# Gathering the first expert group's rows of two tiles in float32, straight from the residual sum

## The chip, the cores and the metric

The kernel runs on one core of a Trainium2 chip. The metric is the device time of one execution in microseconds: the median of several runs. Smaller is better.

## The reference

One layer of a hybrid decoder on 256 prompt tokens and 8 sample tokens, width 1024, all float32. What matters here is its second half:

```python
hres = x + jnp.concatenate([att, conv_y], axis=-1) @ w_out
hn = rmsnorm(hres, g_ffn)
...
lg = (x @ w_rg) + b_rg;  g = jnp.argmax(lg, axis=-1)        # hier_moe(x = hn): 4 groups
le_g = ((x @ w_re) + b_re) of group g                      # 8 experts in each
top_l, top_i = lax.top_k(le_g, 2); w_top = softmax(top_l) * softmax(lg)[g]
h = silu(x @ w_gate[e]) * (x @ w_up[e]) * gates[:, e]       # for each of 32 experts e
y = hres + sum_e h @ w_down[e]
```

The last result is `rmsnorm(y, g_final)`. The weights of the 32 experts are 3 MiB each, 96 MiB in all.

## The kernel before, in words

**Tiles of rows.** The 264 token rows lie in `yres` (128 partitions x 3 x 1024): tiles 0 and 1 are prompt rows, tile 2 the 8 sample rows. They are handled in the order 0, 2, 1, since tile 1's attention and output projection end last.

**The order written out by hand.** `ORDER` (lines 36 to 46) lists named steps; each step is a small function in `steps`, and they are issued in that order, on all engines at once. So each engine works its instructions off in the order of the list. The last three lines of the list hold the stretch that the change touches. Steps that the prediction names, with t the tile, k a column piece, hf a half of the columns:
- `o111`, `o112` and the like (`out_mm`, lines 749 to 760): output projection of tile 1, added to `yres` on VectorE. `o111` and `o112` are the two halves of its last block and write the same PSUM tile.
- `Htk` (`norm2_half`, lines 796 to 820): sum of squares on ScalarE, transposes on TensorE into `xh` with the norm's weight (VectorE), and the float32r rounding `hn` of the rows (ScalarE).
- `Otk` (`norm2_lo`, line 827): the remainder `hlo` = row minus `hn`, on VectorE, for tile 2 on GpSimd. A product with `hn` and one with `hlo` give the float32 result in two float32r products.
- `ltk`, `Rt`, `R1p`, `Lt`: router logits on TensorE, the norm's scale (VectorE, then a power on GpSimd), logits times scale.
- `rat` to `ret` (`route`): the routing in five parts on VectorE. `rct` gives `A` (which two experts a row goes to), `rdt` starts two exponentials on ScalarE, `ret` ends with the gates `G`.
- `rkt`, `oht`: the rank of a row among its expert's rows (TensorE), and the one-hot `Pg` of the slots of the first expert group (VectorE).
- `g00` to `g21` (`gather_mm`, line 987; first digit the tile, second the half of the columns; `h` or `l` behind them is one of the two float32r products): product of one-hot and rows into `px`, so that the 4 x 32 slots of the group get their rows. `ga0` and `ga1` copy the halves of `px` to `xr` (ScalarE and VectorE, lines 998 and 1000), `gt0` and `gt1` transpose them and scale them to `xg` (lines 1016 to 1022).
- `warmi` (`fill`, line 1063): products whose result nobody reads.
- `room` (line 1071): tiles for the weights that are loaded in pieces.

`hn` and `hlo` hold the columns in the order in which the experts' weights want them (eight planes of 128), the residual sum in natural order, so that rounding and remainder also permute. In column order of the weights, neighbours lie 8 floats apart in `yres`.

**Experts.** The 32 experts go in 8 groups of 4. For each group: gate product `pgt` and up product `pup` (line 1149), the gather of the next group (line 987, from `hn` and `hlo`, all tiles), the down product `pyy` (line 1163), and its way back into `yres` (lines 1171 to 1257). Beside the first gate product run `gather_rs` (the slots' scale, `prs`, line 1007) and `slot_maps` (`PGw` on GpSimd, line 1126, which needs `G` and is read by a product on TensorE ahead of the up product).

**Weights.** SyncE issues the loads in a fixed order (lines 1095 to 1122), 1 MiB each, into a ring of 15 slots; a load waits until the last product that read its slot has ended. Group 1's gate weights g10 to g13 take the four slots of the output-projection weights. u02 and u03 (experts 2 and 3, up, group 0) don't go into the ring but in pieces into the tiles `uq` and `uh` that `room` made; u11 goes half into `uh` and half into the slot of g00. In the kernel before, SyncE's order is: group 0 (gate, two up, down), g10 to g13, u02, u03, u10, the two halves of u11, u12, u13, d10 and so on.

Of the kernel before, what the change touches and what calls it, by code (L numbers as in the profile page):

```python
# [85 lines left out]
def hymba_step(ctx: ExitStack, tc: tile.TileContext, x_prompt, x_sample, cache_k, cache_v, state_conv,  # L86
# [35 lines left out]
    with tc.manual_schedule():  # L122
# [673 lines left out]
        def norm2_half(t, k):  # L796

            n = NR[t]
            a, w = COLS[t][k]
            if k == 0:  # L800
                hn[t] = c4(f"hn{t}", [128, 8, 128], F32R)
                if t == 2:

                    P.memset(hn[t][0:40].bitcast(F32), 0.0)
                    hlo[t] = hn[t][32:40]
                else:
                    hlo[t] = c4(f"hlo{t}", [128, 8, 128], F32R)
                ss2[t] = c1(f"ssb{t}", [128, 3])
                xh[t] = c4("xh", [128, 8, 128])
            y = yres[:n, t, a:a + w]  # L810
            S.activation(sqj[:n, 0:w], y, AF.Square, accum_out=ss2[t][:n, k:k + 1])
            pt = ps("pt")
            pv_ = pt.rearrange("p (c n) -> p c n", c=4)
            m, c0 = w // 128, a // 128
            for c in range(m):
                T.transpose(pv_[:, c, 0:n], y[:, 128 * c:128 * c + 128], ident[:n, :n])
            V.tensor_tensor(xh[t][:, c0:c0 + m, 0:n], pv_[:, 0:m, 0:n],
                            gfT[:, c0:c0 + m, None].to_broadcast([128, m, n]), op=OP.mult)
            p = slice(a // 8, (a + w) // 8)
            S.copy(hn[t][:n, :, p].rearrange("t c p -> t p c"), y.rearrange("t (p c) -> t p c", c=8))  # L820

        def norm2_lo(t, k):

            n = NR[t]
            a, w = COLS[t][k]
            p = slice(a // 8, (a + w) // 8)
# [238 lines left out]
        for i in range(3):  # L1065
            steps[f"warm{i}"] = lambda: fill(2)
# [342 lines left out]
```

## Time and profile before

| | us |
|---|---|
| runs, median of 3 | 422.75 |
| lowest and highest | 421.94, 424.46 |
| profiled execution, its own time | 423.49 |
| its span | 421.8 |
| TensorE busy in the span | 382.7 (91%) |
| VectorE, ScalarE, GpSimd busy | 196.4, 92.0, 104.7 |

The span runs from the first to the last instruction of the profiled execution; its own time is 1.7 us longer. In the profile PE is TensorE, PEld its weight loads, DVE is VectorE, ACT ScalarE, POOL GpSimd, SP SyncE, and SPq the queue in which SyncE issues transfers; L987 is line 987 of the kernel. A float32 product of 512 columns appears as two instructions, one of float32r as one. The engines' shares are means over stages with different limits, so they are read stage by stage.

### The profile page before, as it was taken

To read this page: it belongs to the slowest core of one execution; us is meant where nothing else is said; L and a number is where in the kernel's file an instruction comes from. 1 tells how busy PE (TensorE), PEld (TensorE's weight loads), DVE (VectorE), ACT (ScalarE), POOL (GpSimd) and SP (SyncE) were. 2 spreads that over 40 slices of the span, in tenths; PEclk is the share of its full clock that TensorE was granted. 3 is DMA by queue.
4 is the path that set the end of the run, shared out by engine and by line. 5 is a ranking of instruction groups with operands and counts; after the bars stand their busy time and mean duration, and the time that the engine had idled before them with its cause. 6 is when DMAs were issued, how large, how long until landed. Compare 5 with 4: busy or idle time off the path is not lost.

```text
span 421.8 us, 6576 instructions
## 1 busy us (share of the span) xinstructions
PE 382.7 (91%) x2626; PEld 208.0 (49%) x2626; DVE 196.4 (47%) x384; ACT 92.0 (22%) x232; POOL 104.7 (25%) x103
## 2 busy tenths in 40 slices
PE   7899999999999999987999999888699699799980
PEld 6354346678775334464545554443353364354530
DVE  2148987899764033688234343406015016024054
ACT  4120223164340012241320212111011021011032
POOL 3636888978306001030100000000000000000041
PEclk9899999999999999999899999989889789799996
DMA  7999978869987999949699999999999999999922
GB/s 259 416 373 421 367 292 308 340 220 392 424 358 266 421 429 423 409 204 347 234 413 399 425 427 425 426 428 424 428 427 424 427 427 426 427 427 416 401 99 108
DMA packets 32981, 155.04 MB, mean 368 GB/s; under 512 B 3068, under 2 KB 5322, under 8 KB 17972
## 3 DMA queue, kind: packets, MB, share of 16 engines
q1 hardware_dynamic: 27328, 119.69, 70.1%
q0 software_dynamic: 5008, 33.80, 20.3%
q10 hardware_dynamic: 612, 1.11, 0.7%
q8 instruction: 22, 0.36, 0.3%
q14 instruction: 11, 0.09, 0.1%
HBM read 152.40 MB, written 2.20 MB: 367 GB/s over the span
## 4 chain that ended last, share of the span: by engine, by line
PE 42%; DMA 32%; DVE 13%; issue 7%; POOL 3%; ACT 1%; DVEq 0%; ACTq 0%; SPq 0%; POOLq 0%
DMA u<-in_w_up_dram 14%; DMA g<-in_w_gate_dram 9%; DMA d<-in_w_down_dram 8%; PE py L755 4%; PE pup L1149 4%; PE pov L709 3%; PE acck L238 3%; DVE Sd L480 3%; PE accB L552 3%; PE pgt L1149 3%; PE accq L238 3%; PE pyy L1163 3%; PE accv L238 2%; PE px L987 2%; POOL K L474 1%
## 5 line engine op out<-in xcount | busy, mean ns | idle before, releaser
L1149 PE MATMUL pup<-u,xg 128*32 128x256 f32 x472 | 42.9, 468 | 12.2 <-DMA u<-in_w_up_dram 12.2
L1223 DVE SCALAR_TENSOR_TENSOR sh<-pup,rsl,sh 128x256 f32<-128x256 f32 x8 | 5.3, 666 | 90.2 <-PE pup L1149 83.6
L1126 POOL TENSOR_TENSOR PGw<-Pg,G 128x384 f32<-128x384 f32 x8 | 6.9, 857 | 161.0 <-DVE Pg L976 124.4
L474 POOL TENSOR_TENSOR K<-K,qv 128x2048 f32<-128x2048 f32 x9 | 40.7, 4536 | 6.3 <-DMA K<-in_cache_k_dram,idx 4.5
L480 DVE TENSOR_REDUCE Sd<-K 128x32 f32<-128x2048 f32 x16 | 35.9, 2277 | 4.7 <-POOL K L474 4.6
L1149 PE MATMUL pgt<-g,xg 128*32 128x256 f32 x512 | 32.5, 394 | 3.5 <-DMA g<-in_w_gate_dram 2.4
L1149 PEld LDWEIGHTS pup<-u,xg 128*32 128x32 f32 x472 | 19.2, 133 | 32.0 <-DMA u<-in_w_up_dram 16.3
L1163 PE MATMUL pyy<-d,hT 128*32 128x512 f32 (+1 forms) x272 | 30.9, 579 | 0.6 <-DVE hT L1243 0.6
L755 PE MATMUL py<-wo,mixT 128*128 128x512 f32 (+1 forms) x72 | 29.0, 550 | 1.1 <-DVE yres L760 1.1
L1180 PE MATMUL pz<-Y,PT 128*128 128x512 f32 (+1 forms) x90 | 26.7, 421 | 0.7
L1149 PEld LDWEIGHTS pgt<-g,xg 128*32 128x32 f32 x512 | 16.5, 113 | 18.4 <-DMA g<-in_w_gate_dram 3.8
L1257 DVE TENSOR_TENSOR yres<-yres,pz 128x512 f32<-128x512 f32 (+1 forms) x42 | 25.6, 670 | 0.0
L1172 DVE SCALAR_TENSOR_TENSOR Y<-pyy,gsl,Y 128x512 fp32r<-128x512 f32 (+1 forms) x17 | 12.2, 720 | 25.5 <-ACT Y L1171 25.5
L998 ACT COPY xr<-px 128x512 f32<-128x512 f32 (+1 forms) x16 | 8.8, 557 | 68.0 <-PE px L987 68.0
L987 PE MATMUL px<-hn,Pg 128*128 128x512 f32 (+1 forms) x48 | 21.9, 480 | 0.1
L1171 ACT ACTIVATE Y<-pyy,gsl 128x512 fp32r<-128x512 f32 (+1 forms) x17 | 11.3, 663 | 48.3 <-PE pyy L1163 48.3
L1180 PEld LDWEIGHTS pz<-Y,PT 128*128 128x128 f32 (+1 forms) x90 | 12.1, 154 | 18.0 <-ACT Y L1171 6.4
L303 POOL DMA_INDIRECT V<-in_cache_v_dram,idx x16 | 15.1, 944 | 22.2 <-PE pov L709 18.2
L755 PEld LDWEIGHTS py<-wo,mixT 128*128 128x128 f32 x72 | 13.3, 190 | 13.5 <-issue 11.8
L303 POOL DMA_INDIRECT K<-in_cache_k_dram,idx x16 | 15.7, 982 | 12.4 <-DMA K<-in_cache_k_dram,idx 5.6
L1163 PEld LDWEIGHTS pyy<-d,hT 128*32 128x32 f32 x272 | 8.3, 111 | 17.7 <-issue 16.1
L238 PE MATMUL accq<-wq,xnT 128*128 128x512 f32 x32 | 16.3, 657 | 0.3 <-DVE xnT L221 0.3
(334 smaller groups left out, 612.0 us busy)
## 6 DMA issues: line engine op xcount, KB each, us to landing
g<-in_w_gate_dram SPq DMA_DIRECT2D x32, 1024.0 KB, 19.6
d<-in_w_down_dram SPq DMA_DIRECT2D x28, 1024.0 KB, 19.6
u<-in_w_up_dram SPq DMA_DIRECT2D x25, 1024.0 KB, 19.5
u<-in_w_up_dram SPq DMA_DIRECT2D x9, 512.0 KB, 14.2
wo<-in_w_out_dram SPq DMA_DIRECT2D x4, 1024.0 KB, 15.1
wk<-in_w_in_dram SPq DMA_DIRECT2D x2, 1024.0 KB
wv<-in_w_in_dram SPq DMA_DIRECT2D x2, 1024.0 KB, 30.6
wC<-in_w_in_dram SPq DMA_DIRECT2D x2, 1024.0 KB
```

What stands on the lines that cost most here:

```text
L238: T.matmul(acc, lhsT=xnT[:, cc, 128 * t:128 * t + 128], rhs=W[pn, kk][:, c, :], start=cc == 0, stop=cc == 7)
L303: P.indirect_dma_start(out=t, out_offset=None, in_=src, in_offset=bass.IndirectOffsetOnAxis(ap=idx[:, b, hh:hh + 1], axis=0))
L474: P.tensor_tensor(kslots[i], kslots[i], qv[:, None, :].to_broadcast([128, 4, 512]), op=OP.mult)
L480: V.tensor_reduce(Sd[:, b, 4 * hh:4 * hh + 4, :].rearrange("p i h -> p (i h)"), kslots[i].rearrange("p i (h d) -> p (i h) d", h=8), axis=A ...
L552: T.matmul(acc[:, 0:264], lhsT=W[pn, kk][:, c, 128 * m:128 * m + 128], rhs=xnT[:, cc, 0:264], start=cc == 0, stop=cc == 7)
L709: T.matmul(po[32 * j:32 * j + 32], lhsT=pvs[b // 4][:, b % 4, i, :], rhs=vslots[2 * b + i // 4][:, i % 4, :], start=s == 0, stop=s == 1, t ...
L755: T.matmul(po[:, lo:lo + w], lhsT=mixT[:, c, 128 * t:128 * t + 128], rhs=wo[n, c // 4][:, c % 4, lo:lo + w], start=c == 0, stop=c == 7, sk ...
L987: T.matmul(PX[grp, hf], lhsT=PgS[grp][:n, POS[t]].rearrange("p j s -> p (j s)"), rhs=(hn, hlo)[low][t][:n, 4 * hf:4 * hf + 4, :].rearrange ...
L1149: T.matmul(dst[32 * j:32 * j + 32, 0:256], lhsT=xg[:, c, 32 * j:32 * j + 32], rhs=w[:, 256 * k:256 * k + 256], start=c == 0, stop=c == 7, ...
L1163: T.matmul(py[32 * j:32 * j + 32, 0:w], lhsT=hT[:, c, 32 * j:32 * j + 32], rhs=dw[grp, j][:, 1024 * c + a:1024 * c + b], start=c == 0, sto ...
L1180: T.matmul(pz, lhsT=PTS[grp][:, 128 * t:128 * t + NR[t]], rhs=Y[:, i, 0:w], start=start and i == 0, stop=i == 1, skip_group_check=more)
L1257: V.tensor_tensor(yv, yv, pz[:m], op=OP.add)
```

## The change

For tiles 1 and 2 the rows of the first expert group are gathered by float32 products straight from `yres`, read in the weights' column order (stride 8). Tile 0 still uses `hn` and `hlo`. The rounding and remainder of tiles 2 and 1, which the later groups use, become two steps `hl2` and `hl1` at the end of the list (ScalarE and VectorE, two pieces of 512 columns each; none on GpSimd any more). In the list `re0` moves up behind `rd0`, `re2` and `re1` behind `gt1`; `H12` is cut in two and `R1` is put between the parts; three pairs of warm-up products become a pair and a single one. On SyncE u02 and u03 are loaded ahead of g13 in place of behind it.

```diff
-H21 l20 R2 g00 O20 l21 O21 L2 ra2 rb2 room g01 o111 rc2 l10 O10 o112 H11 R1p H12 rk2 oh2 R1 O11 l11 l12 L1 ra1 rb1 rc1
-g20 warm0 g21 warm1 rk1p rk1 warm2 oh1 O12 rd2 g10h g11h re0 g10l ga0 g11l ga1 re2 gt0 gt1 rd1 re1
+H21 l20 R2 g00 l21 L2 ra2 rb2 room g01 o111 rc2 l10 o112 H11 R1p H12a R1 H12b rk2 oh2 l11 l12 L1 ra1 rb1 rc1
+g20 warm0 g21 rk1p rk1 warm1 oh1 rd2 g10 ga0 g11 ga1 gt0 gt1 rd1 re2 re1 hl2 hl1
...
+            return pv_
+        def norm2_x(t, k, pv_):
...
             V.tensor_tensor(xh[t][:, c0:c0 + m, 0:n], pv_[:, 0:m, 0:n],
                             gfT[:, c0:c0 + m, None].to_broadcast([128, m, n]), op=OP.mult)
-            p = slice(a // 8, (a + w) // 8)
-            S.copy(hn[t][:n, :, p].rearrange("t c p -> t p c"), y.rearrange("t (p c) -> t p c", c=8))
+            if t == 0:
+                norm2_hi(t, a, w)
+        def norm2_hi(t, a, w):
+            n, p = NR[t], slice(a // 8, (a + w) // 8)
+            S.copy(hn[t][:n, :, p].rearrange("t c p -> t p c"),
+                   yres[:n, t, a:a + w].rearrange("t (p c) -> t p c", c=8))
+        def norm2_both(t):
+            for a in (0, 512):
+                norm2_hi(t, a, 512)
+                norm2_lo(t, a, 512)
...
-            (P if t == 2 else V).tensor_tensor(
+            V.tensor_tensor(
                 hlo[t][:n, :, p], yres[:n, t, a:a + w].rearrange("t (p c) -> t c p", c=8),
                 hn[t][:n, :, p].bitcast(F32), op=OP.subtract)
...
+                steps["H12a"] = lambda: late.append(norm2_half(1, 2))
+                steps["H12b"] = lambda: norm2_x(1, 2, late[0])
+            if t:
+                steps[f"hl{t}"] = lambda t=t: norm2_both(t)
...
             for t in tiles:
+                if grp == 0 and t:
+                    n = NR[t]
+                    T.matmul(PX[grp, hf], lhsT=fl(PgS[grp], t, n).bitcast(F32),
+                             rhs=yres[:n, t, :].rearrange("t (p c) -> t c p", c=8)[:, 4 * hf:4 * hf + 4, :],
+                             start=False, stop=t == 1)
+                    continue
...
-        for i in range(3):
-            steps[f"warm{i}"] = lambda: fill(2)
+        for i in range(2):
+            steps[f"warm{i}"] = lambda i=i: fill(2 - i)
...
                 for j in range(4):
+                    if (grp, nm, j) == (1, "g", 3):
+                        for k in (2, 3):
+                            load_split(0, "u", k, uw, wu_v)
...
-                if (grp, nm) == (1, "g"):
-                    for j in (2, 3):
-                        load_split(0, "u", j, uw, wu_v)
```

## Rows read from the trace of the kernel before

**Rows 1.** Busy time by stretch: stretch, its length, then for PE, PEld, DVE, ACT and POOL busy us and (instructions), then the granted TensorE clock (1.00 is 2.4 GHz, 0.50 is 1.2 GHz), the DMA engines' busy share and GB/s.
```profile
184.00:189.00 5.00, 3.86 (x22) 3.17 (x21) 4.69 (x14) 1.03 (x3) 1.67 (x2) 1.00 0.07 26
204.00:207.00 3.00, 3.00 (x39) 1.95 (x31) 0.00 (x0) 0.59 (x2) 0.43 (x1) 1.00 0.10 30
212.00:222.00 10.00, 9.76 (x63) 5.16 (x63) 3.32 (x6) 2.70 (x5) 0.00 (x0) 1.00 1.00 399
242.00:400.00 158.00, 141.56 (x1234) 73.06 (x1230) 44.91 (x73) 21.09 (x46) 4.17 (x5) 0.91 1.01 424
```

**Rows 2.** The waits of SyncE's queue over the whole run: engine line, waited for what: us in total, times, longest us. (The first is the wait for the slot of the last output-projection weight; the row names the next instruction on TensorE that signalled.)
```profile
SPq L1110 <- PE pt L816: 12.3, 3, 11.9
...
SPq L1081 <- PE pgt L1149: 10.1, 1, 10.1
```

**Rows 3.** The timeline of SyncE, its issues: start us, us over all, engine line operation, out<-in, count.
```profile
189.26 2.04 SPq L1081 DMA_DIRECT2D uq<-in_w_up_dram  x4
...
205.53 0.33 SPq L1081 DMA_DIRECT2D u<-in_w_up_dram  x1
```

**Rows 4.** The chain of waits, pieces in order of time: start us, us, what.
```profile
156.53 3.44 PE py L755 x8
...
200.48 5.03 PE pgt L1149 x64
...
207.72 3.59 PE pup L1149 x64
211.31 3.29 PE px L987 x10
```

**Rows 5.** The timeline of VectorE: start us, us, engine line operation, out<-in, shapes, count, and in brackets, where there was any, the idle time before it and what ended it. The routing of the sample tile (183 to 185 us), the last piece of tile 1's second norm and what stands behind it (190 us), the same two routing steps for tile 1 (192 us), and the first and last of the eight instructions of gate step re0 and the first of re2's.
```profile
183.10 1.12 DVE L899 SCALAR_TENSOR_TENSOR rcols<-L,rcols,tab 128x4 f32<-128x4 f32 x1
...
184.45 1.27 DVE L906 SCALAR_TENSOR_TENSOR l<-rcols,L 128x32 f32<-128x32 f32 x1
...
189.80 0.42 DVE L817 TENSOR_TENSOR xh<-pt,rowsT 128x256 f32<-128x256 f32 x1
...
190.55 0.29 DVE L976 TENSOR_TENSOR Pg<-rka,tab 128x128 fp32r<-128x128 f32 x1
190.76 0.15 DVE L857 SCALAR_TENSOR_TENSOR rs<-ssb,rs 128x1 f32<-128x1 f32 x1
...
192.31 0.22 DVE L899 SCALAR_TENSOR_TENSOR rcols<-L,rcols,tab 128x4 f32<-128x4 f32 x1
...
192.76 0.25 DVE L906 SCALAR_TENSOR_TENSOR l<-rcols,L 128x32 f32<-128x32 f32 x1
...
196.67 0.15 DVE L936 RECIPROCAL rcols<-rcols 128x1 f32<-128x1 f32 x1
...
197.90 0.19 DVE L943 TENSOR_TENSOR G<-rcols 128x32 f32<-128x32 f32 x1
...
198.67 0.15 DVE L936 RECIPROCAL rcols<-rcols 128x1 f32<-128x1 f32 x1
```

**Rows 6.** The timeline of GpSimd, same columns.
```profile
182.67 3.00 POOL L827 TENSOR_TENSOR hn<-yres,hn 8x512 fp32r<-8x512 f32 x2
191.05 0.74 POOL L858 TENSOR_TENSOR rsb<-rs,mhalf 128x1 f32<-128x1 f32 x1 [5.39 <-DVE rs L857]
...
203.41 1.02 POOL L1126 TENSOR_TENSOR PGw<-Pg,G 128x384 f32<-128x384 f32 x1 [11.55 <-DVE G L943]
```

**Rows 7.** The timeline of TensorE, same columns.
```profile
184.69 0.98 PE L837 MATMUL pl<-wr,xh 128*128 128x36 f32 x8
186.81 1.99 PE L755 MATMUL py<-wo,mixT 128*128 128x256 f32 x8 [1.14 <-DVE yres L760]
...
191.38 1.13 PE L1063 MATMUL warm<-yres,ident 128*128 128x256 f32 x4
...
193.84 0.30 PE L954 MATMUL prk<-A,onesb__72 128*128 128x32 bf16 x2
194.88 0.18 PE L961 MATMUL prk<-A,trib 128*128 128x32 bf16 x1 [0.74 <-DVE A L922]
...
195.75 0.71 PE L987 MATMUL px<-hn,Pg 128*128 128x512 f32 x2
196.30 0.64 PE L987 MATMUL px<-hlo,Pg 128*128 128x512 f32 x2
...
198.48 0.87 PE L1016 MATMUL pxt<-ident,xr 128*128 128x128 f32 x6 [0.62 <-DVE xr L1000]
```

**Rows 8.** The timeline of ScalarE, same columns.
```profile
189.68 0.19 ACT L811 ACTIVATION_READ_ACCUMULATOR Sd<-yres 128x1 f32 x1
...
206.39 0.16 ACT L1009 COPY rsl<-prs 128x1 f32<-128x1 f32 x1 [4.51 <-PE prs L1007]
```

**Rows 9.** VectorE's groups by line and shape between 120 and 245 us: line engine operation, out<-in, shapes, count, then busy us, mean ns of one, and the idle time before them.
```profile
L827 DVE TENSOR_TENSOR hlo<-yres,hn 128x512 fp32r<-128x512 f32 x3 | 3.3, 1090 | 0.0
...
L817 DVE TENSOR_TENSOR xh<-pt,rowsT 128x512 f32<-128x512 f32 x3 | 2.0, 678 | 0.0
```

**Rows 10.** Busy time by stretch, columns as in rows 1: the half microsecond in which the granted clock fell.
```profile
199.50:200.00 0.50, 0.00 (x0) 0.00 (x0) 0.43 (x3) 0.00 (x0) 0.00 (x0) 0.89 0.93 393
```

**Rows 11.** ScalarE's groups of the same stretch, same columns as in rows 9.
```profile
L820 ACT CAST hn<-yres 128x512 fp32r<-128x512 f32 x3 | 3.2, 1076 | 0.0
...
L769 ACT COPY yq<-py 128x512 f32<-128x512 f32 x2 | 1.2, 585 | 1.1 <-PE py L243 1.1
```

More of the change, by code (lines that the diff above doesn't have):

```diff
@@ L42 @@
 cv2 b3 B10 b2 V3 cv0 V0 c2 c3 ov V2 V1 B13 eB1 G25 o010 kvs o000 eB3 G26 eB0 G27 G28 G29 o110 G30 V5 eB2 X0 V4
-o001 V6 H00 G31 o011 V7 H01 X1 pe l00 o100 R0 l01 L0 ra0 rb0 O00 rc0 o101 as rk0 O01 co rd0 z0 z1 y0 oh0 H10 y1 H20
-H21 l20 R2 g00 O20 l21 O21 L2 ra2 rb2 room g01 o111 rc2 l10 O10 o112 H11 R1p H12 rk2 oh2 R1 O11 l11 l12 L1 ra1 rb1 rc1
-g20 warm0 g21 warm1 rk1p rk1 warm2 oh1 O12 rd2 g10h g11h re0 g10l ga0 g11l ga1 re2 gt0 gt1 rd1 re1
+o001 V6 H00 G31 o011 V7 H01 X1 pe l00 o100 R0 l01 L0 ra0 rb0 O00 rc0 o101 as rk0 O01 co rd0 re0 z0 z1 y0 oh0 H10 y1 H20
+H21 l20 R2 g00 l21 L2 ra2 rb2 room g01 o111 rc2 l10 o112 H11 R1p H12a R1 H12b rk2 oh2 l11 l12 L1 ra1 rb1 rc1
+g20 warm0 g21 rk1p rk1 warm1 oh1 rd2 g10 ga0 g11 ga1 gt0 gt1 rd1 re2 re1 hl2 hl1
 """
@@ L816, in norm2_half, with norm2_lo @@
                 T.transpose(pv_[:, c, 0:n], y[:, 128 * c:128 * c + 128], ident[:n, :n])
+            return pv_
+        def norm2_x(t, k, pv_):
+            n = NR[t]
+            a, w = COLS[t][k]
+            m, c0 = w // 128, a // 128
             V.tensor_tensor(xh[t][:, c0:c0 + m, 0:n], pv_[:, 0:m, 0:n],
                             gfT[:, c0:c0 + m, None].to_broadcast([128, m, n]), op=OP.mult)
-            p = slice(a // 8, (a + w) // 8)
-            S.copy(hn[t][:n, :, p].rearrange("t c p -> t p c"), y.rearrange("t (p c) -> t p c", c=8))
[L822 to L826, printed above, removed]
-            (P if t == 2 else V).tensor_tensor(
+            if t == 0:
[8 more added lines that the diff above has]
+                norm2_lo(t, a, 512)
+        def norm2_lo(t, a, w):
+            n, p = NR[t], slice(a // 8, (a + w) // 8)
+            V.tensor_tensor(
                 hlo[t][:n, :, p], yres[:n, t, a:a + w].rearrange("t (p c) -> t c p", c=8),
@@ L866, in hymba_step @@
             for k in range(len(COLS[t])):
-                steps[f"H{t}{k}"] = lambda t=t, k=k: norm2_half(t, k)
+                steps[f"H{t}{k}"] = lambda t=t, k=k: norm2_x(t, k, norm2_half(t, k))
                 steps[f"l{t}{k}"] = lambda t=t, k=k: norm2_log(t, k)
-                steps[f"O{t}{k}"] = lambda t=t, k=k: norm2_lo(t, k)
+                if t == 0:
+                    steps[f"O{t}{k}"] = lambda t=t, k=k: norm2_lo(t, *COLS[t][k])
             steps[f"R{t}"] = lambda t=t: norm2_rs(t)
@@ L872, in hymba_step @@
                 steps["R1p"] = lambda: norm2_pre(1)
+                steps.pop("H12")
+                late = []
+                steps["H12a"] = lambda: late.append(norm2_half(1, 2))
+                steps["H12b"] = lambda: norm2_x(1, 2, late[0])
+            if t:
+                steps[f"hl{t}"] = lambda t=t: norm2_both(t)
             steps[f"L{t}"] = lambda t=t: norm2_L(t)
@@ L1054, in hymba_step @@
         for hf in range(2):
-            for low in range(2):
-                steps[f"g1{hf}" + "hl"[low]] = lambda hf=hf, low=low: gather_mm(0, hf, (1,), (low,))
+            steps[f"g1{hf}"] = lambda hf=hf: gather_mm(0, hf, (1,))
             steps[f"ga{hf}"] = lambda hf=hf: gather_rows(0, hf)
```

1 line of the change is left out of this document (added).

## The prediction

> **What bounds the kernel now.** I read the view by stretches first, then SyncE's waits and issues, then the chain, then the timelines of the stretch that these point to. From 242 to 400 us the DMA engines are full (share 1.01, 424 GB/s), and from 212 on they are nearly so (399 GB/s) [rows 1]. That second half is a stream of weights of fixed size, so it ends as early as it begins. It begins late: from 204 to 207 us the engines move 30 GB/s [rows 1], because SyncE has waited 10.1 us for one thing, the end of the first group's gate product, whose weights sit in the slots that the next weights want [rows 2]; at 205.53 the queue moves again [rows 3]. The chain has this product from 200.48 to 205.51 [rows 4]. So a change before 205.5 us is worth what it moves the end of that product, if nothing behind it slips. A second hole, 26 GB/s from 184 to 189 us [rows 1], is SyncE waiting 11.9 us for the slot of the last output-projection weight [rows 2]; it costs nothing as long as what is loaded there arrives before it is used.
>
> **Routing of the sample tile.** Two of VectorE's routing instructions take 1.12 and 1.27 us there; the same lines take 0.22 and 0.25 for tile 1 [rows 5]. At that time GpSimd runs O20 and O21, 3.00 us from 182.67 on [rows 6]. The change takes these two from GpSimd, which gives VectorE 0.90 + 1.02 = 1.92 us. The residual add of o111 stands behind them, and TensorE's o112 waits 1.14 us for that add [rows 7]. TensorE's work in between, l10, ends at 184.69 + 0.98 = 185.67, which is now the limit: o112 starts at 185.67 for 186.81, **1.14 us** earlier, not 1.92.
>
> **Norm of tile 1.** The square of its last piece ends at 189.87 [rows 8], but R1 starts on VectorE at 190.76, behind the scaled copy of H12, two rank copies and a one-hot [rows 5]. The change splits H12 and puts R1 ahead of these. The square now ends 1.14 earlier, 188.73; with 0.15 for R1, the 0.14 to GpSimd's start at 191.05 (190.76 + 0.15 to 191.05) and 0.74 for the power [rows 5, 6] the scale is there at 189.8, 2.0 us earlier than 191.79. R1 delays the scaled copy to 188.9, and from that copy's start to the one-hot's end are 1.04 us (189.80 to 190.84) [rows 5]: 189.95, no later than the scale. The logits follow: **1.9 us** earlier in all. O10 and O11 (1.09 us for 512 columns [rows 9]) leave VectorE here too; O10 ended just as the add behind it became due, so I cost its removal at nothing.
>
> **TensorE before the last rank.** The routing instructions of tile 1 keep their length, so their result A, ready for 194.88 [rows 7], is ready for 192.95. TensorE has to be there: from 190.0 it has g20, warm0, g21 and the rank's start. In float32 a 512-column product is two instructions, 3.44 us for eight [rows 4], 0.43 each, so g20 and g21 take 0.86 us each where float32r takes about 0.33 (ten in 3.29 us) [rows 4]. 190.0 + 0.86 + 1.13 + 0.86 + 0.30 [rows 7] = 193.15: the rank is at 193.2, and 0.2 us of the gain is lost. The single warm-up product left behind the rank still fits before g10.
>
> **Gather of tile 1.** From the rank to g10's start stay 0.87 us (194.88 to 195.75) [rows 7]: 194.07. g10 ends 0.86 + 0.07 later, at 195.0, g11 at 195.86. Before, the high parts ran at 195.75 and the low parts, behind O12, at 196.30 to 196.94 [rows 7]; float32 costs TensorE the same here. The gain lies on VectorE. The eight instructions of re0 (196.67 to 198.09) stood ahead of the copies out of PSUM, and TensorE waited 0.62 us for those; the eight of re2 (from 198.67) stood ahead of the scaling [rows 5, 7]. re0 moves to where ScalarE's exponentials of tile 0 are long done and VectorE waits for the sample tile; re2 moves behind the scaling. Now TensorE goes on from g11 into the transposes of half 0, four at 0.145 us (0.87 for six) [rows 7], 196.45, half 1 is copied by 196.3 and transposed by 197.05, and the gate product starts at **197.1 for 200.48: 3.4 us**.
>
> **The clock.** The gate product takes 5.03 us and the up product of the same size 3.59 [rows 4]. The granted clock fell just before it (0.89 in the half microsecond from 199.5, in which TensorE did nothing) [rows 10]. In the new order TensorE's idle times from 193.2 to 197.1 add up to some 0.5 us, so I take it that the clock stays at 2.4 GHz, 3.59 us: the product ends at 200.7 for 205.51, **4.8 us** earlier.
>
> **The strided read.** The float32 products read the residual rows 32 bytes apart. No row shows TensorE doing that. VectorE needs 1.09 us with such a read against 0.68 packed [rows 9], ScalarE 1.08 with a strided write against 0.59 [rows 11]. Bounds for one pass are then 0.43 (nothing lost) and 1.09 (VectorE's whole time). I take 0.43: a float32 pass already spends two cycles of 2.4 GHz on a column (0.43 us for 512), so a read at half pace would still keep up. The Trainium skill, SBUF — State Buffer, section "Door 1: The DMA port swizzle", speaks against the change: an access that crosses into a new 16-byte line pays a penalty, and here each one does. The other engines' rows agree, none shows it for TensorE, and by it the gain would be 1.4 and not 4.2 us, the second rival below.
>
> **Work moved under the product.** hl2 and hl1 put four casts on ScalarE (1.08 each, 4.3 us) [rows 11] and four subtractions on VectorE (4.4 us) [rows 9], two of these GpSimd's before. ScalarE was idle 4.51 us there [rows 8]; now it casts from 198.6 to 202.9, so the copy of the slots' scale, due at 201.6, is 1.3 us late, and what is behind it ends some two us before the up product does. VectorE does rd1, re2 and re1 until 201.0, subtracts until 205.4 and makes the next one-hot by 206.0; the next gather needs it 5.8 us after the gate product (205.51 to 211.31) [rows 4], at 206.5. Without that cover up to 4.4 us would come back. GpSimd's PGw (1.02 us) [rows 6] waits for re1 and must be done 1.4 us after the gate product, at 202.1. Alone it would be at 202.2. Beside a subtraction it can lose one whole one, 1.09, as VectorE lost 0.90 to GpSimd above. Between 0.1 and 1.2 I take **0.6 us** lost. It is on the path, because the down weights behind it wait for slots: the engines ran below full then (399 GB/s) [rows 1].
>
> **The loads.** The split loads of u02 and u03 pass g13, whose slot wait held them until 189.26 [rows 3]. The last user of their own slots is l21, which the list has ahead of o111, so 2 MiB fall into the empty stretch, and g13, u10 and the half of u11 follow when o112 ends, at 187.7; group 1 uses those after 216. Six issues pass one on SyncE, none is added. I cost this at nothing: it covers the up product, now due at 203.
>
> **Sum.** 4.8 - 0.6 = 4.2 us. The profiled execution is 423.49 us (span 421.8), so 419.3; it stands 0.74 above the median of the runs, 422.75, and against the median I forecast **418.6 us**.
>
> **Rivals.**
> - *The clock falls again.* TensorE idles less, but the rows show one fall and not where another order would put it. The gate product keeps its 5.03 us: gain 4.2 - 1.4 = 2.8, 419.95. Chance 0.15.
> - *The strided read costs TensorE what it costs ScalarE in proportion* (1.08/0.59, 0.79 us a pass). With p for a pass the rank is at 191.43 + 4p and the gate product at that + 2.18 + 4p, once p is over 0.38. For p = 0.79 that is 199.9, the end 203.5, gain 2.0 - 0.6 = 1.4: 421.4. Chance 0.15. The rule of the Trainium skill's page SBUF — State Buffer, named above, would act like this.
> - *Slower: a pass costs VectorE's 1.09 us or more.* The place is the same; the gate product starts at 202.3 and ends at 205.9, 1.0 late with the 0.6: 423.8, and 425.2 if the clock falls too. It turns the change into a loss from p = 0.96 on. For it: a row read 32 bytes apart cost VectorE that. Over 0.5% slower it is from p = 1.23 on. Against: VectorE loses a good third of its pace, and the same share makes only 0.7 of a pass. Chance 0.09.
> - *The cover fails*: the casts or subtractions run late and the next gather or the slots' scale waits 1 to 2.5 us more: 419.6 to 421.1. Chance 0.08. The Trainium skill, SBUF — State Buffer, section "Who interferes with whom", says that an instruction of VectorE with two SBUF inputs and one of GpSimd exclude each other for a whole instruction; the 1.12 us above agrees, and by it the 0.6 would be 1.2 and the forecast 419.2.
> - *It does nothing measurable*, because the stream does not begin earlier for a reason I don't see: 422.75. Chance 0.06.
>
> **Chances.** The forecast has 0.47. Over 0.5% (2.1 us, about what a measurement of this kernel can tell from no change) faster: the forecast 0.47, 0.13 of the clock, 0.07 of the cover, 0.03 of the strided read, 0.70. Slower by over 0.5%: 0.06 of the dear pass. Within: the rest, 0.24. Range 417.1 (nothing lost behind the product, and as far below the median as the fastest run, 0.8) to 421.9 (the proportional strided read and the runs' spread).
>
> **What would show it.** In the changed profile the two instructions take about 0.22 and 0.25 us; o112 has no wait for a VectorE add; float32 gather instructions follow each other by 0.43; the gate product starts near 197.1, lasts 3.6 at a granted 1.00, and SyncE's next issue is near 200.7; uq and uh issue before 184; PGw ends by 203. Passes over 0.9 us, a gate product of 5 us, or a gap ahead of the next gather would make the number wrong.

## The result

| | before | after |
|---|---|---|
| runs of one comparison, median | 423.28 (9 runs) | 425.97 (9 runs) |
| lowest and highest | 421.94, 426.29 | 422.89, 427.74 |
| profiled execution, its own time | 423.49 | 427.74 |
| its span | 421.8 | 425.7 |
| mean granted clock | 0.951 | 0.939 |

The ratio is 1.0059, with a 95% interval of 1.0033 to 1.0085: **slower by 0.6%**, 2.7 us, where 4.2 us of gain were forecast. The forecast was 418.6 with a range of 417.1 to 421.9; the time lies above the range, and it moved the other way.

### The profile page after: what moved, and what is told of

Its sections match the earlier page's. It is cut to its first block, busy times and chain, and to the rows that moved or that the text cites. A ratio compares the mean times of both kernels' runs of the same rounds, so it can differ in the third digit from the quotient of the medians.

```text
span 425.7 us, 6567 instructions
## 1 busy us (share of the span) xinstructions
PE 389.4 (91%) x2622; PEld 209.2 (49%) x2622; DVE 197.3 (46%) x385; ACT 92.4 (22%) x231; POOL 102.3 (24%) x101
## 4 chain that ended last, share of the span: by engine, by line
PE 43%; DMA 29%; DVE 11%; issue 8%; POOL 6%; ACT 1%; DVEq 0%; POOLq 0%; ACTq 0%; SPq 0%
DMA u<-in_w_up_dram 14%; PE pup L1178 6%; PE py L755 6%; DMA K<-in_cache_k_dram,idx 5%; DMA g<-in_w_gate_dram 5%; DMA d<-in_w_down_dram 5%; PE px L1017 4%; PE pyy L1192 4%; PE pov L709 3%; DVE Sd L480 3%; PE accB L552 3%; PE pgt L1178 3%; POOL K L474 2%; PE px L1011 2%; POOL K L303 2%
## 5 line engine op out<-in xcount | busy, mean ns | idle before, releaser
L1178 PE MATMUL pup<-u,xg 128*32 128x256 f32 x472 | 45.1, 477 | 12.2 <-DMA u<-in_w_up_dram 12.2
L1155 POOL TENSOR_TENSOR PGw<-Pg,G 128x384 f32<-128x384 f32 x8 | 7.5, 932 | 165.3 <-DVE Pg L999 124.0
L1178 PE MATMUL pgt<-g,xg 128*32 128x256 f32 x512 | 31.1, 381 | 2.0 <-DMA g<-in_w_gate_dram 1.8
L1017 PE MATMUL px<-hn,Pg 128*128 128x512 f32 (+1 forms) x44 | 20.2, 481 | 0.0
```

Of the source, the lines that this page charges most:

```text
L1017: T.matmul(PX[grp, hf], lhsT=PgS[grp][:n, POS[t]].rearrange("p j s -> p (j s)"), rhs=(hn, hlo)[low][t][:n, 4 * hf:4 * hf + 4, :].rearrange ...
L1178: T.matmul(dst[32 * j:32 * j + 32, 0:256], lhsT=xg[:, c, 32 * j:32 * j + 32], rhs=w[:, 256 * k:256 * k + 256], start=c == 0, stop=c == 7, ...
```

## The profile after

In the profiled execution of after the attention stage ends 0.89 us later than in that of before (the first of its last products, line 243, starts at 174.79 for 173.90). Times below are the trace's own; where they are set against before, 0.89 is taken off and the text says so.

Busy time by stretch, columns as in [rows 1]:

```profile
184.00:189.00 5.00, 4.71 (x28) 4.00 (x27) 3.15 (x14) 0.58 (x3) 0.00 (x0) 1.00 1.00 335
192.80:203.00 10.20, 10.20 (x22) 4.83 (x22) 2.89 (x15) 1.14 (x5) 0.00 (x0) 0.50 0.46 193
209.90:213.20 3.30, 3.30 (x33) 1.56 (x36) 2.52 (x3) 0.90 (x4) 0.65 (x1) 0.50 1.01 384
222.00:232.00 10.00, 9.91 (x104) 4.46 (x96) 5.54 (x9) 1.57 (x3) 0.83 (x1) 1.00 0.73 287
242.00:400.00 158.00, 142.56 (x1210) 72.38 (x1212) 46.30 (x75) 21.78 (x47) 4.16 (x5) 0.91 1.01 425
```

See three things. The stretch from 184 to 189 us, nearly empty in [rows 1], is full. TensorE's clock is at its lower level, 0.50, for 10.2 us before the gate product and again for 3.3 us behind it; TensorE is busy all that time, at half pace. And a hole that before did not have opens from 222 to 232 us (287 GB/s). From 242 on the two kernels are alike.

SyncE's wait for the gate product and its longest waits for the down and the up product (columns as in [rows 2]), and its issues (as in [rows 3]):

```profile
SPq L1110 <- PE pgt L1178: 16.1, 1, 16.1
...
SPq L1142 <- PE pyy L1192: 14.1, 2, 8.4
...
SPq L1142 <- PE pup L1178: 9.6, 3, 6.1
```

```profile
178.06 2.42 SPq L1110 DMA_DIRECT2D uq<-in_w_up_dram  x4
...
207.08 0.33 SPq L1110 DMA_DIRECT2D u<-in_w_up_dram  x1
...
208.46 16.24 SPq L1142 DMA_DIRECT2D d<-in_w_down_dram  x4
224.79 7.08 SPq L1142 DMA_DIRECT2D g<-in_w_gate_dram  x4
```

The queue moves again at 207.08, 206.19 with the 0.89 off: 0.66 late against the 205.53 of [rows 3], not 4.8 early. Then the four down loads take 16.24 us to issue: they wait 6.1 us for the up product, and the last of them 8.4 us for the end of the *down* product of the first group. The loads of group 2 follow at 224.79. That is the hole.

The timeline of TensorE (columns as in [rows 7]); line 1011 is the new float32 gather, 1178 the gate product:

```profile
186.41 1.97 PE L755 MATMUL py<-wo,mixT 128*128 128x256 f32 x8
...
190.74 2.08 PE L1011 MATMUL px<-yres,Pg 8*128 8x512 f32 x2
192.75 2.07 PE L1092 MATMUL warm<-yres,ident 128*128 128x256 f32 x4
194.75 2.18 PE L1011 MATMUL px<-yres,Pg 8*128 8x512 f32 x2
...
197.14 0.21 PE L984 MATMUL prk<-A,trib 128*128 128x32 bf16 x1
...
198.18 3.86 PE L1011 MATMUL px<-yres,Pg 128*128 128x512 f32 x4
...
203.41 3.66 PE L1178 MATMUL pgt<-g,xg 128*32 128x256 f32 x64
...
209.03 0.91 PE L1166 MATMUL pgs<-ones__71,PGw 128*128 128x1 f32 x6 [0.59 <-POOL PGw L1155]
```

The two passes of g20 take 2.0 us (190.74 to 192.75) with the clock still at 2.4 GHz (granted 1.00 up to 192.7); the warm-up pair, 1.13 us in [rows 7], takes 2.0 at 1.2 GHz; the four passes of g10 and g11 start 0.92 us apart (198.18 to 201.86). So the last rank runs at 197.14. The chain of waits behind it (as in [rows 4]):

```profile
209.94 5.24 PE pup L1178 x64
215.18 3.29 PE px L1017 x10
220.79 3.69 PE pyy L1192 x32
```

The up product takes 5.24 us for the 3.59 of [rows 4]. VectorE, GpSimd and ScalarE (columns as in [rows 5, 6, 8]):

```profile
183.95 0.22 DVE L922 SCALAR_TENSOR_TENSOR rcols<-L,rcols,tab 128x4 f32<-128x4 f32 x1
...
184.40 0.25 DVE L929 SCALAR_TENSOR_TENSOR l<-rcols,L 128x32 f32<-128x32 f32 x1
...
193.58 0.25 DVE L945 SCALAR_TENSOR_TENSOR A<-rcols 128x32 bf16<-128x32 f32 x1
197.39 0.19 DVE L989 SCALAR_TENSOR_TENSOR rka<-prk,A 128x32 f32<-128x32 f32 x1 [3.56 <-PE prk L984]
...
207.23 2.59 DVE L843 TENSOR_TENSOR hn<-yres,hn 8x512 fp32r<-8x512 f32 x2
209.85 2.10 DVE L843 TENSOR_TENSOR hlo<-yres,hn 128x512 fp32r<-128x512 f32 x2
```

```profile
207.34 1.64 POOL L1155 TENSOR_TENSOR PGw<-Pg,G 128x384 f32<-128x384 f32 x1 [16.92 <-DVE G L966]
```

```profile
204.79 3.89 ACT L831 CAST hn<-yres 8x512 fp32r<-8x512 f32 x4
```

A is there at 193.83, 192.94 with the offset off, as forecast (192.95); then VectorE waits 3.56 us for TensorE.

For all kernels that follow, the profiled execution is cut at three marks: **P**, the start of the first product of the last attention projection; **G**, the end of the gate product; **D**, the end of the first group's down product. From D to the moment at which 140 of the 148 MiB have been moved the trace gives 165.3 to 166.0 us in each of the profiles below: what a kernel does ahead of D reaches the end only by moving D.

| | P | G - P | D - G | D - P | median, ratio to before |
|---|---|---|---|---|---|
| before | 173.90 | 31.61 | 14.98 | 46.59 | |
| b_again1 | 173.98 | 30.27 | 14.97 | 45.25 | |
| b_again2 | 176.49 | 30.26 | 15.00 | 45.26 | |
| after | 174.79 | 32.28 | 17.29 | 49.57 | 425.97, 1.0059 [1.0033, 1.0085] |
| a_again | 174.92 | 31.77 | 17.34 | 49.11 | |
| e1_packed | 176.09 | 28.42 | 15.65 | 44.07 | 423.17, 1.0004 [0.9978, 1.0030] |
| e2_copy | 174.40 | 29.58 | 17.27 | 46.85 | 423.09, 0.9996 [0.9972, 1.0020] |
| e3_order | 174.69 | 28.63 | 14.98 | 43.61 | 421.46, 0.9972 [0.9955, 0.9989] |
| f1_pgw | 176.47 | 28.47 | 14.91 | 43.37 | 422.39, 0.9981 [0.9955, 1.0007] |
| f2_warm | 173.18 | 31.42 | 17.34 | 48.76 | 425.19, 1.0059 [1.0035, 1.0082] |
| f3_sample | 174.49 | 30.81 | 14.90 | 45.72 | 422.24, 0.9993 [0.9974, 1.0011] |
| f4_scale | 174.67 | 28.26 | 15.00 | 43.26 | 421.91, 0.9976 [0.9948, 1.0004] |
| f5_rows40 | 173.54 | 28.02 | 14.90 | 42.92 | 420.66, 0.9954 [0.9923, 0.9985] |
| f6_rows128 | 173.91 | 27.42 | 14.90 | 42.32 | 419.30, 0.9926 [0.9898, 0.9954] |
| g1_all | 174.61 | 26.88 | 14.92 | 41.81 | 419.31, 0.9901 [0.9862, 0.9940] |
| l1_loads | 174.74 | 31.75 | 15.00 | 46.75 | 423.94, 1.0027 [1.0000, 1.0054] |

A profile is one execution: P alone wanders by 3 us, and what follows the 140 MiB by nearly 4. So D - P tells what a step did in that execution, and the median whether it holds. The profiled execution of after is the slowest of its nine runs, that of e1_packed the slowest of its twelve (426.86).

## Experiments

**The price of the read (t1_table).** The kernel before, with a table of float32 products of 512 columns ahead of the last group's up product: neighbouring columns 4, 8, 16 and 32 bytes apart, first over 128 rows and then over 8, six products (twelve passes) of each.

```diff
+for nr in (128, 8):
+    for sd in (1, 2, 4, 8):
...
+        for _ in range(6):
+            T.matmul(pt_, lhsT=ident[:nr, :], rhs=src, start=True, stop=True)
```

> The kernel before, with a table of float32 products of 512 columns put in ahead of the last group's up product, results unused: six each with 128 and with 8 rows of the moving operand, read 4, 8, 16 and 32 bytes apart. Only their spacing in the trace is of interest, not the time of the run. Theory READ (reading 32 bytes apart starves TensorE): a pass of 512 columns takes 0.43 us packed and about 1.0 us at 32 bytes, at either clock, with 8 rows as with 128; somewhere between for 8 and 16 bytes. Rival CLOCK (the read costs little; the passes of 1.0 us in the changed kernel are passes at the low clock): 0.43 at every distance at 2.4 GHz, 0.85 at 1.2 GHz.

The table's products alone by stretch; columns are the stretch, its length, then PE, PEld and DVE busy us and (instructions), granted clock, DMA share and GB/s. 128 rows at 4, 8, 16 and 32 bytes, then 8 rows at 8 and at 32 bytes:

```profile
394.46:399.62 5.16, 5.16 (x13) 2.29 (x14) 0.00 (x0) 1.00 1.07 389
399.62:405.02 5.40, 5.40 (x14) 2.26 (x12) 0.00 (x0) 1.00 0.57 198
405.02:415.80 10.78, 10.78 (x14) 2.47 (x12) 0.00 (x0) 1.00 0.00 0
415.80:426.92 11.12, 11.12 (x13) 2.29 (x12) 0.00 (x0) 1.00 0.00 0
...
436.12:446.36 10.24, 10.24 (x14) 3.96 (x13) 0.00 (x0) 0.50 0.00 0
...
457.16:468.35 11.19, 11.19 (x13) 3.37 (x11) 0.00 (x0) 0.50 0.00 0
```

Each stretch is the start of one set to that of the next, so a twelfth of it is a pass: 0.43, 0.45, 0.90 and 0.93 us at a granted 1.00. At 1.2 GHz (8 rows) 8 bytes cost 0.85, twice as much, but 32 bytes still 0.93. READ is right: the strided pass has one price at either clock, so here the clock is not what bounds it. The Trainium skill, SBUF — State Buffer, section "Door 1: The DMA port swizzle", says that a 16-byte line wants two hits for full bandwidth; the rows agree (two floats of a line used, 0.45; one, 0.90). It also says that float32 may be read four apart for free; that is the 0.90 row, so here the measurement decides against it. CLOCK has a point too: the clock fell at 428.18, 1.26 us into the products of 8 rows, and stayed low through all of them, while it had held through the 128-row ones.

**The read undone in the changed kernel (e1_packed).** The gather reads packed rows, so the columns come in the wrong order and the permutation is left out.

```diff
-rhs=yres[:n, t, :].rearrange("t (p c) -> t c p", c=8)[:, 4 * hf:4 * hf + 4, :],
+rhs=yres[:n, t, 512 * hf:512 * hf + 512],
```

> The changed kernel with the float32 gather reading the same rows packed, 512 neighbouring columns, so the rows come out in the wrong column order (the permutation is left out); the count and size of all instructions stay. READ: passes of 0.43 us, the clock stays up through the gather, the gate product starts near 197 to 198 us and ends near 201 to 202; 419 to 421 us. CLOCK: the 8-row products and the missing warm-up products let the clock fall near 193 us as in the changed kernel, passes of 0.85, gate product from 201 on; 424 to 426 us.

423.17 us, between what READ (419 to 421) and CLOCK (424 to 426) expected: 2.8 us come back by the medians, 2.3 by the ratios, and G - P falls by 3.9; but no gain over before is left. TensorE's gathers (g20; then g10 and g11):

```profile
192.05 1.12 PE L1011 MATMUL px<-yres,Pg 8*128 8x512 f32 x2
...
196.49 3.07 PE L1011 MATMUL px<-yres,Pg 128*128 128x512 f32 x4
```

At full clock the pass of 8 rows is 0.53 here; g10 and g11 ran mostly at 1.2 GHz (low from 195.46 to 198.88), 0.73 a pass.

**The same with the permutation kept (e2_copy).** ScalarE copies the rows in weight order into a packed float32 tile, which the gather reads; everything else as in the change.

```diff
+S.copy(hp[t][:n, :, p].rearrange("t c p -> t p c"),
+       yres[:n, t, a:a + w].rearrange("t (p c) -> t p c", c=8))
...
+rhs=hp[t][:n, 4 * hf:4 * hf + 4, :].rearrange("t c p -> t (c p)"),
```

> The changed kernel with one thing added: ScalarE first copies the rows of tiles 2 and 1 in float32 into the weights' column order, where the kernel before made the float32r part, and the float32 gather reads that copy packed. It computes the whole reference. READ: as the packed kernel, at most 0.5 us later, since the copies (0.62 to 1.08 us each) run on ScalarE beside the routing: 419 to 421 us. CLOCK: no better than the changed kernel, 424 to 426 us.

423.09: as e1_packed, and again 2 us above what READ expected. So undoing the read is worth 2 to 3 us, and something else holds back the 4 that were forecast. Part of it shows in the passes of g10 and g11: they ran at 1.2 GHz (low from 193.09 to 199.91), and a packed pass then takes 0.85 us (195.33 to 198.74 for four), little less than the strided 0.92. The low clock hides part of what the packed read saves.

**The moved routing alone (e3_order).** The kernel before with two steps moved:

```diff
-... co rd0 z0 ... g10h g11h re0 g10l ga0 g11l ga1 re2 gt0 gt1 rd1 re1
+... co rd0 re0 z0 ... g10h g11h g10l ga0 g11l ga1 gt0 gt1 rd1 re2 re1
```

> The kernel before with one part of the change alone: the gate steps re0 and re2 leave the stretch between the gather and the first gate product (re0 moves up behind rd0, re2 behind the scaling), the gather stays in float32r with remainders, the warm-ups and loads stay. If VectorE's queue there is what holds the gate product, it starts near 199.0 for 200.5 us and the time is 1.4 us shorter (421.5 to 422), 2.8 shorter if the clock then doesn't fall before it. If the copies out of PSUM were not held by VectorE, no difference.

421.46, a gain of 0.28%, and the interval stays below 1. The transposes of the gathered rows:

```profile
198.24 1.34 PE L1016 MATMUL pxt<-ident,xr 128*128 128x128 f32 x8 [0.48 <-ACT xr L998]
```

The eight run through; VectorE's copy, for which [rows 7] have a wait of 0.62 us, holds TensorE up no more (the 0.48 for ScalarE's copy stay). That step of the prediction was right.

**The clash of PGw (f1_pgw).** e2_copy with the first group's PGw on VectorE ahead of the subtractions.

```diff
-... rd1 re2 re1 hl2 hl1
+... rd1 re2 re1 pgw hl2 hl1
+V.tensor_tensor(gates[0], PgS[0].bitcast(F32), G[...].to_broadcast([128, 3, 4, 32]), op=OP.mult)
```

> The changed kernel with the packed float32 copy (as in e2_copy), and the first group's PGw computed by VectorE behind re1 and ahead of hl2, in place of GpSimd beside hl2's subtractions. CLASH theory: the subtractions held GpSimd up (1.69 us where it took 1.02), TensorE stood 0.58 us ahead of pgs, and that pause let the clock fall in the up product. Then PGw takes under 0.9 us, pgs waits for nothing, the up product takes 3.6 to 3.7 us, and the first group's down product ends 15.4 us or less behind the gate product (17.7 in e2_copy): about 421 us, 0.5% below e2_copy's 423.1. Rival, EARLIER CLOCK: the fall in the up product follows from what TensorE did before 200 us, not from this pause: up product 5.2 us, 422.5 or more.

e2_copy first (PGw on GpSimd, then pgs, then the up product in the chain), then f1_pgw:

```profile
204.18 1.69 POOL L1166 TENSOR_TENSOR PGw<-Pg,G 128x384 f32<-128x384 f32 x1 [13.27 <-DMA uh<-in_w_up_dram]
...
205.92 0.91 PE L1177 MATMUL pgs<-ones__71,PGw 128*128 128x1 f32 x6 [0.58 <-POOL PGw L1166]
```

```profile
206.84 5.24 PE pup L1189 x64
```

```profile
205.12 0.56 DVE L1114 TENSOR_TENSOR PGw<-Pg,G 128x384 f32<-128x384 f32 x1
...
206.23 0.91 PE L1185 MATMUL pgs<-ones__71,PGw 128*128 128x1 f32 x6
```

```profile
207.14 3.59 PE pup L1197 x64
```

PGw takes 0.56 us, pgs waits for nothing, D - G falls from 17.27 to 14.91. CLASH is right about the wait, but the time, 422.39, is above its 421: the medians differ by 0.7 us, less than the two intervals together can tell. That the wait lets the clock fall is likely and not shown: it fell in the up product in four of the five profiles with the wait (after, a_again, e2_copy, f2_warm, not e1_packed), and in none of those without. f1_pgw by itself does not refute EARLIER CLOCK, since its clock had been low ahead of the gate product only from 195.86 to 199.28, about as in e1_packed; in the four with the fall it was low twice as long or longer. f3_sample, below, speaks against it: its clock was low as long as e2_copy's (193.12 to 199.94), pgs does not wait, and the up product takes 3.69 us.

**More warm-up products (f2_warm).** e2_copy with the three pairs of before.

```diff
-g20 warm0 g21 rk1p rk1 warm1 oh1
+g20 warm0 g21 warm1 rk1p rk1 warm2 oh1
```

> The changed kernel with the packed float32 copy (as in e2_copy), and with the three pairs of warm-up products of the kernel before in their old places (the changed kernel has one pair and a single one). WARM theory: the clock fell at 193 us because TensorE had fewer full products ahead of the last rank: with three pairs it stays at 2.4 GHz from 190 us to the gate product, which then starts 0.5 to 1 us earlier against the attention stage than in e2_copy; about 422.3. Rival, SMALL ROWS: the float32 products of 8 rows do not hold the clock whatever stands between them: it falls between 191 and 196 us all the same, the added pairs then run at 1.2 GHz (1.0 us each more), and the last rank is as late or later: 423 to 424.

425.19: 2.1 us slower than e2_copy. WARM falls. From 191.4 to 198.1 (columns as in [rows 1]) the clock is low all the same, and the added pairs run at half pace:

```profile
191.40:198.10 6.70, 6.70 (x14) 3.70 (x15) 1.79 (x11) 0.39 (x3) 0.00 (x0) 0.50 0.54 180
```

**R1 ahead (f4_scale)** adds to e3_order the split of H12 with R1 between the parts.

```diff
-R1p H12 rk2 oh2 R1 O11
+R1p H12a R1 H12b rk2 oh2 O11
```

> e3_order (the kernel before with re0 behind rd0 and re2 behind gt1) and, further, the change's split of H12 with R1 between the parts. If that step of the prediction was right by itself, R1 starts some 0.75 us earlier, the scale and A follow by 0.7 us, and the gate product starts 0.7 us earlier than in e3_order: 420.8, 0.5% below the kernel before. Rival: TensorE or VectorE has other work there, and nothing is gained over e3_order's 421.5.

In the profile G - P is 0.4 less than in e3_order, of the 0.7 expected; the median, 421.91, is 0.45 more. Not settled: too small for these runs.

**The sample tile (f3_sample).** f4_scale, with the sample tile alone gathered in float32 from a packed copy, 8 rows, and PGw on VectorE.

```diff
-H21 l20 R2 g00 O20 l21 O21 L2 ...  gt0 gt1 rd1 re2 re1
+H21 l20 R2 g00 l21 L2 ...          gt0 gt1 rd1 re2 re1 pgw hl2
+T.matmul(PX[grp, hf], lhsT=fl(PgS[grp], t, 8).bitcast(F32), rhs=hp[t][:8, ...], ...)
```

> f4_scale and, further, the sample tile's rows for the first group gathered in float32 from a packed copy (8 rows, no subtraction on GpSimd beside the routing), its rounding and remainder made behind re1, and PGw on VectorE; prompt tiles as in the kernel before (float32r), three pairs of warm-up products. If the routing's 1.14 us come through and the clock holds, the gate product starts about 1.8 us earlier than in e3_order and the time is 419.5 to 420. SMALL ROWS theory: the four float32 passes of 8 rows let the clock fall around 193 us, the pairs of warm-ups run at 1.2 GHz, and the gain over f4_scale is lost: 421 to 422.5.

422.24, as SMALL ROWS expected; the medians do not tell it from f4_scale's 421.91, but G - P is 30.81 for 28.26, though the routing is quicker. By then each of the seven profiles with float32 products of 8 rows (after, a_again, e1, e2, f1, f2, f3) had a fall of the clock between 191 and 196 us, and none of the six without (before three times, l1, e3, f4).

**The rows filled up (f5_rows40, f6_rows128).** The same with zeros below the 8 rows, so that the product is over 40 or 128 rows. The lines of f6_rows128:

```diff
+P.memset(hp[t][0:128], 0.0)
-lhsT=fl(PgS[grp], t, 8).bitcast(F32), rhs=hp[t][:8, ...]
+lhsT=fl(PgS[grp], t, 128).bitcast(F32), rhs=hp[t][:128, ...]
```

> f3_sample with the sample tile's float32 products over 40 rows in place of 8 (32 of them zeros), as many rows as the float32r products of the kernel before have. ROWS theory: the 8 rows let the clock fall; with 40 it holds as it does in the kernel before: no fall between 190 and 200 us, the gate product starts 2 to 3 us earlier against the attention stage than in f3_sample (27.1 us from there to its start), about 420. Rival, PASSES: four float32 passes let it fall whatever their rows: a fall near 193 us and 422.2 as f3_sample.

> The same over all 128 rows (120 of them zeros). ROWS theory: as f5_rows40 or better, no fall between 190 and 200 us, gate product end about 28 us behind the attention stage's last products (30.8 in f3_sample), about 420. Rival, PASSES: 422.2.

420.66 and 419.30; against f3_sample, 422.24, that is 1.6 and 2.9 us. The two do not differ by more than their intervals, and neither has a fall of the clock between 190 and 270 us. TensorE from g20 on and the stretch in which the clock had fallen, f3_sample and then f6_rows128:

```profile
192.62 1.62 PE L1010 MATMUL px<-hp,Pg 8*128 8x512 f32 x2
194.16 2.08 PE L1092 MATMUL warm<-yres,ident 128*128 128x256 f32 x4
```

```profile
193.20:199.90 6.70, 6.70 (x17) 3.96 (x15) 2.15 (x11) 0.48 (x4) 0.00 (x0) 0.50 0.97 378
```

```profile
191.75 1.02 PE L1011 MATMUL px<-hp,Pg 128*128 128x512 f32 x2
192.60 1.03 PE L1093 MATMUL warm<-yres,ident 128*128 128x256 f32 x4
```

```profile
193.20:199.90 6.70, 6.12 (x65) 3.75 (x68) 4.93 (x26) 3.17 (x14) 0.00 (x0) 1.00 1.02 409
```

The same instructions, passes and order but for the writing of the zeros, 120 rows more, and the clock stays at 2.4 GHz until 271 us. ROWS is right, PASSES falls. The two passes of g21 take no longer for it: 0.85 us over 128 rows (191.75 to 192.60), 1.05 over 8 rows at full clock (e1_packed, 194.16 to 195.21) and over 40 (f5_rows40, 191.68 to 192.73).

**The three causes taken away (g1_all).** f1_pgw with the 128 rows of f6_rows128; all else is the change.

> The changed kernel with the packed float32 copy, PGw on VectorE (both as in f1_pgw) and, further, the sample tile's float32 products over 128 rows (120 of them zeros). THREE CAUSES: these are all that was wrong with the forecast; no fall of the clock between 190 and 210 us, the gate product ends some 27.4 us behind the first product of the last attention projection (f6_rows128) or a little earlier, the first down product 14.9 later, and the time is 418.6 to 419.5. Rival, A FOURTH: something else of the change (its fewer warm-up products, its order of loads, the four casts and subtractions on the way to the next gather) still costs a microsecond or more: 420.5 or more.

419.31, 1.0% below before, 4.1 us; G - P is the shortest of all. The four passes of g10 and g11:

```profile
194.59 1.96 PE L1024 MATMUL px<-hp,Pg 128*128 128x512 f32 x4 [0.17 <-DVE Pg L1012]
```

THREE CAUSES holds: no fall of the clock between 190 and 210 us, D - P 41.81, where the forecast's 4.2 us off before's 46.59 would make 42.39. So the profile has no room for a fourth; the median's interval alone (2.5 to 5.8 us below before) would not rule one out. f6_rows128 gives the same time, as far as these runs can tell, with prompt tiles in float32r, so the float32 gather of tile 1 is not needed for it.

**The order of loads alone (l1_loads).** The kernel before, with u02 and u03 ahead of g13 as in the change's diff.

> The kernel before with the change's order of loads alone (u02 and u03 ahead of g13). The prediction costs it at nothing. CHAIN theory: the stream of weights is bound twice, by the end of the first gate product and then by the end of the first group's down product, which frees the next slots; what is loaded earlier only moves the empty time of the DMA engines, so 184 to 189 us fill up, a hole of about the same size opens later, and the time is that of the kernel before within 0.3%: 422 to 424. Rival, LOADS: the 2 MiB that now come before 189 us compete with something or let the stream start ahead, and the time moves by 1 us or more either way.

Busy time by stretch, columns as in [rows 1]:

```profile
184.00:189.00 5.00, 3.87 (x22) 3.42 (x22) 4.69 (x13) 1.03 (x3) 2.50 (x2) 1.00 0.93 311
199.00:204.00 5.00, 3.54 (x34) 1.93 (x38) 4.19 (x25) 1.42 (x7) 0.00 (x0) 0.70 0.02 7
```

The first stretch fills and a new hole opens before the gate product ends; D - P, 46.75, is that of before's first profile, both with a fall of the clock in the gate product (5.16 and 5.03 us). CHAIN holds as to the profile; by the median it may cost up to 0.5% (the interval is 1.0000 to 1.0054), which these runs leave open.

**Both kernels once more (b_again1, b_again2, a_again)**, without an edit.

> The kernel before, unchanged, profiled once more. CHANCE theory: the fall of the clock in the gate product (1.4 us of 5.03) is not in each execution, so the profile that the prediction rests on showed a saving of 1.4 us that is mostly not there: here the gate product takes 3.6 to 3.7 us or the fall lies elsewhere, and the down product of the first group ends 45 to 45.5 us behind the first product of the last attention projection (46.6 in the first profile). Rival, FIXED: the fall is at the same place again, 5.0 us.

> The same once more: as for b_again1, CHANCE says that the length of the gate product differs from one execution to another between 3.66 and some 5 us; FIXED says 5.0 us each time.

> The changed kernel, unchanged, profiled once more. READ says that the float32 passes from rows read 32 bytes apart take 0.9 to 1.0 us again, CHANCE that the places at which the clock falls differ from the first profile, so that the up product takes 3.66 or up to 5.3 us; the down product of the first group then ends 48 to 49.6 us behind the first product of the last attention projection (49.57 in the first profile).

The gate product in the chain of b_again1, and of b_again2:

```profile
200.59 3.66 PE pgt L1149 x64
```

```profile
203.09 3.66 PE pgt L1149 x64
```

3.66 us both times, where [rows 4] have 5.03: CHANCE is right. The fall that the prediction meant to save is not in every execution (it came again in l1_loads, not in e3_order). The Trainium skill, TensorE: Matmul & The Clock Gate, section "Part 1: The HAM clock gate (the "warmup" mystery)", says of the rise to the higher clock that its moment varies from run to run of one kernel. The three profiles of before show the like of a fall: one has it at 199.89 us, the other two have none between 190 and 270. a_again had the strided passes at 0.92 and 1.0 us, the clock low from 193.36 to 200.18 and in the up product again, D - P 49.11: both profiles of after have both falls.

## Why the prediction was wrong

The step that failed is **the strided read**: "I take 0.43". A pass from rows 32 bytes apart takes 0.92 to 1.0 us (t1_table, the profile after), near the upper bound of 1.09 and not at the lower. The reason given, that the read would still keep up with a float32 pass, is what the table refutes: at 8 bytes it does (0.45), at 16 the price has doubled (0.90). The eight passes took 7.8 us (4.13 and 3.68) where the sum has 3.44. The rival "a pass costs VectorE's 1.09 us or more", with 0.09, had the place and the mechanism; but by its own sum (the gate product starts at 193.61 + 8p) a pass of 0.93 to 1.0 us comes out even, between 0.3 faster and 0.3 slower, so the read alone does not make the loss of 2.7. Two more steps failed: the clock, by the medians worth as much as the read, and what a wait behind the gate product can cost.

In the profile D - P is 49.57, 7.2 us more than the 42.39 of the forecast. Of these, 5.5 lie ahead of the end of the gate product (206.18 with the offset off, for 200.7) and 1.7 behind it. Term by term:

- **Bounds.** Right that what moves the gate product moves the end "if nothing behind it slips". What was not seen is how little it may slip: about six loads of 1 MiB are queued behind the gate product, some 15 us of stream at the 424 GB/s of [rows 1], and the down product that frees the next slots ends 15.0 us behind it. In after that part grew from 14.98 to 17.29 us, and the hole at 222 us opened.
- **Routing of the sample tile.** Right: 0.22 and 0.25 us, and o112 at 186.41 without a wait, 1.29 earlier with the offset off (1.14 forecast).
- **Norm of tile 1.** Right: A 1.9 us earlier, as forecast.
- **TensorE before the last rank.** Forecast 193.2 for the rank; it ran at 197.14, or 196.25 with the offset off. The four passes of 8 rows make some 2.4 of this (4.1 for 1.72) and the warm-up pair at 1.2 GHz 0.9; g20 began 0.15 early.
- **Gather of tile 1.** Right in its order: e3_order's move alone is worth 1.2 us by the ratio, 1.7 by the medians. Wrong in the price of its passes: 3.68 for 1.72 us.
- **The clock.** "The clock stays at 2.4 GHz" failed twice. The float32 products of 8 rows let it fall ahead of the rank, which no row of before could show, since there the products of this tile run over 40 rows, in float32r; filling the rows up gains 1.6 to 2.9 us (f5, f6 against f3). The rival "The clock falls again", with 0.15, put the fall into the gate product; that ran at full clock, 3.66 us, and the falls lay ahead of it and behind it. And the 1.4 us booked as gain came from one execution: in two of three the gate product of before takes 3.66 us anyway.
- **Work under the product.** The size was right, 0.6: PGw took 1.64 for 1.02 us and pgs waited 0.59; the 1.2 that the prediction gives beside it did not come. Not seen was the up product behind it, which ran at the low clock and took 1.65 us more; it did so in four of the five profiles with this wait and in none without. The cover held: the next gather waited for neither casts nor one-hot.
- **The loads.** Not refuted: l1_loads alone is 0.3% slower, and its interval begins at nothing.

By the medians, the steps from after to g1_all are 2.9 us for the read (after to e2_copy), 0.7 for PGw (to f1_pgw, not told from nothing) and 3.1 for the rows (to g1_all). They are taken off in this order; read and low clock hide part of each other, so another order would share the 6.7 us out otherwise. g1_all is then 4.1 below before; the forecast had 4.2. The agreement is partly luck, since 1.4 of the forecast was a fall of the clock that two of three profiles of before do not have.

## What to carry over

Before a product reads its moving operand in place with a stride, measure one pass at that stride by itself: here columns 8 bytes apart cost almost nothing (0.45 for 0.43 us) and 16 bytes apart doubled the pass, and a packed copy on an idle engine was the cheaper way. Where TensorE's clock matters, fill a product of few rows up with zeros: here its passes took no longer for it, and over 40 and 128 rows the clock held where over 8 it fell. Before you count on winning back a fall of the clock, see whether a second profile of the same kernel has it. And where transfers wait for two events in turn, look at both: e2_copy ended the gate product earlier than any of the three profiles of before (G - P 29.58), lost 2.3 us up to the down product (D - G 17.27), and gained nothing.

## What was not expected of the hardware

- A float32 pass of 512 columns over 128 rows took 0.43, 0.45, 0.90 and 0.93 us with columns 4, 8, 16 and 32 bytes apart; the last hardly changes with the clock (at 1.2 GHz 0.93 over 8 rows in the table, 0.92 over 128 in after), the packed one doubles (0.85 in e2_copy).
- Back-to-back float32 products over 8 rows did not hold TensorE's clock: it fell to 1.2 GHz 1.26 us after they began and stayed there for 40 us while TensorE was busy without a break. In the kernel, products of the same length filled up with zeros to 40 or 128 rows held it (f5_rows40, f6_rows128). Why rows matter is open; the runs show only that they do, for 8 against 40 and 128.
- Whether a pause of 0.6 us is by itself enough for the fall in the up product is open as well: it followed in four profiles of five.
